# One pair of groups of the up projections token-major, parked sums in three steps, the mixing matrix loaded at another place

## The chip, the cores and the metric

The kernel runs on one core of a Trainium2 chip. The time is that of the device in microseconds (us), the median of several executions. Engines are named as in the profile: PE is TensorE's matmul stream and PEld its weight loads, DVE is VectorE, ACT is ScalarE, POOL is GpSimd and SP is SyncE. Times inside the kernel are microseconds from the start of the profiled span.

## The reference

Two layers of an encoder run over 256 tokens of width 2048 in float32. Layer 0 mixes tokens with a gated MLP over blocks of 128 positions, layer 1 with latent attention. Behind each mixer stands a gated MLP with a causal convolution of width 3, which is where most of the change lies:

```python
def conv_ffn(x, w_up, conv_w, conv_b, w_down):      # D_FF = 5504
    h = x @ w_up                                      # 256 x 2048 by 2048 x 11008
    C = h.shape[-1]
    h = lax.conv_general_dilated(h, conv_w[:, None, :], window_strides=(1,),
                                 padding=[(CONV_W - 1, 0)],
                                 dimension_numbers=('NWC', 'WIO', 'NWC'),
                                 feature_group_count=C) + conv_b
    a, g = jnp.split(h, 2, axis=-1)
    return (jax.nn.silu(g) * a) @ w_down

# token mixer of layer 0, the part with the mixing matrix w
w = w_s * mask[None]                                  # 8 matrices of 128 x 128, masked by blocks of 64
s = jnp.einsum('gij,bnjgd->bnigd', w, v) + jnp.transpose(b_s)[None, None, :, :, None]
return (u * s.reshape(B, S, GM_HALF)) @ w_out
```

Each sub-layer is followed by x <- LayerNorm(ALPHA * x + sublayer(x)).

## The kernel before

**Weights.** All weights are read once, in chunks of 128 rows by 2048 columns of float32 (1 MB), in an order that a list `chunks` fixes for the whole kernel. A class `Feed` loads each chunk on SP's queue into one of three `raw` tiles, and splits it: ScalarE rounds it into `wh` (L127) and VectorE takes the rest, `wl` = raw - wh (L130). The parts stand in the 14 slots named `big`. TensorE multiplies with three products: the activation's high and low part by wh, and its high part by wl. `feed.next()` gives the parts of the next chunk and starts loads and splits of later ones.

**Two orientations.** In the *feature-major* form of an up group (`prod_a`, tile `up`), a weight block of 128 x 128 is the stationary side and the 256 tokens are the moving one: 512 columns for wh (high and low tokens side by side) and 256 for wl. A group has four PSUM banks of 128 features each, two for `a` and two for the gate `g`, and goes through four chunks of four blocks of 128 rows; a group of four chunks has 64 matmuls with 512 moving columns and 64 with 256. The two halves of a bank are then added (`sum_halves`, L388 on ScalarE and L390 on VectorE, tile `h`), convolved (tile `c`, L960 to L963) and gated (tile `act`, L978), a pair of `a` and `g` at a time. In the *token-major* form (`prod_b`, used by the gated mixer's v and u stages, class `Banks`) 128 tokens are the stationary side and 512 weight columns move. There a chunk has two blocks of rows by 1024 columns and is either "wide" (`eight`, 24 matmuls of 512 columns) or in seven products (`seven`, 21 matmuls). The latter is Strassen's scheme in Winograd's form: ScalarE and VectorE make sums `ts` of the weight's quarters (L137) and split them into `th` and `tl` (L127, L130), and the activations have sums of their own (`combine`). `rest` puts the banks together at the end. The eight PSUM banks of such a group are q3, p2, e, q4 (`DIRECT`) and p1, q5, p7, p6 (`OWN`).

**Up projections.** Group 0 of a layer is a special one (`upf`), and groups 1 to 21 follow in a loop over `gi`, with chunks in sequence. Beside them run other jobs, taken up at fixed places in the loop: the gates of the group before, the making of the down projection's activation sums, and the *parked sums*. Of eight chunks per layer of the down projection the parts in seven products are made ahead, during the up groups: `park` loads the chunk (`praw`) on POOL's queue, makes its two pairs of parts on ScalarE and VectorE (tiles `pwh`, `pwl`, `pth`, `ptl`) and stores them to DRAM (`kept...`). It is a generator and does one step per call of `next(jobs)`. The tiles come from the six slots named `side`.

**Order.** The program is written in an order which a scheduler turns into one sequence per engine. `pin` keeps an instruction in the order of the program; `behind` puts one after the last matmul written so far, in the scheduler's order, with no semaphore. The engines then wait for each other only where data or buffers ask for it.

**The start.** TensorE runs ten warm-up matmuls over a tile `idle` of zeros. The v stage begins as soon as the first half of chunk 0 is there. The mixing matrix is loaded on POOL's queue in four tiles `wT` (L811), each followed by a clear of its masked quarter (L812), and is first used by the row sums at 52 us.

## Time and profile before

| what | value |
|---|---|
| median of 3 executions | 2463.76 us (2462.9 to 2464.14) |
| the profiled execution | 2463.38 us, span 2461.6 us |
| granted TensorE clock | 1.000 |
| busy: PE, DVE, ACT, POOL | 2453.6, 2071.6, 1498.8, 110.6 us |
| up groups 1 to 21, layer 0 and layer 1 | about 807 to 1275 us and 1767 to 2235 us |
| groups 8 and 9, layer 0 and layer 1 | 968.90 to 1013.35 us and 1928.96 to 1973.41 us |
| v stage (token-major) | about 6 to 256 us |

In the profile's lists a group of instructions is given as line, engine, operation, output<-inputs, shapes and count, then busy time and mean duration in ns, then the idle time of the engine before them and what ended it. In lists by time, the first two columns are start and length in us, and idle time stands in brackets. Matmuls overlap: one with 512 moving columns lasts 0.39 us, while the next starts 0.227 us after it.

### The profile page before, as it was taken

The numbers are of one execution on the slowest core, as the hardware profiler recorded it, in microseconds if no ns is written. First come the engines' busy times: TensorE is split into PE (matmuls) and PEld (weight loads), VectorE is DVE, ScalarE is ACT, GpSimd is POOL, SyncE is SP. The second block draws the span as 40 slices with busy tenths as digits, with TensorE's granted clock in tenths as the row PEclk, the third lists the DMA queues.
The fourth block names the chain that finished last, engine by engine and source line by source line (L and its number), as shares of the span: only waits on it lengthen the run. The fifth ranks groups of instructions, "written<-read, shape, count | busy, mean of one in ns | idle before, by whom it ended". The sixth has DMA issues, their size and how long they took to land. (4 is left out here: it accounts for less than half of the span.)

```text
span 2461.6 us, 32571 instructions
## 1 busy us (share of the span) xinstructions
PE 2453.6 (100%) x12475; PEld 2087.7 (85%) x12475; DVE 2071.6 (84%) x2739; ACT 1498.8 (61%) x2024; POOL 110.6 (4%) x214
## 2 busy tenths in 40 slices
PE   9999999999999999999999999999999999999999
PEld 7888888888888888888888888988888888888887
DVE  7999889989898788787777897868797787878798
ACT  6666777766466656656554566665665565555453
POOL 0000000000000000000001000000000000000000
PEclk9999999999999999999999999999999999999999
DMA  7556665658776778777868885443578787877885
GB/s 285 196 206 215 230 200 192 221 169 310 239 273 240 258 276 330 282 276 304 318 226 316 301 303 186 173 171 126 205 282 309 261 317 292 295 265 281 297 322 202
DMA packets 118156, 624.52 MB, mean 254 GB/s; under 512 B 10840, under 2 KB 11104, under 8 KB 75376
## 3 DMA queue, kind: packets, MB, share of 16 engines
q1 hardware_dynamic: 90128, 462.47, 53.1%
q0 software_dynamic: 27872, 159.97, 17.0%
q8 instruction: 98, 1.61, 0.3%
q14 instruction: 58, 0.48, 0.1%
HBM read 551.04 MB, written 71.35 MB: 253 GB/s over the span
## 5 line engine op out<-in xcount | busy, mean ns | idle before, releaser
L130 DVE TENSOR_TENSOR wl<-raw,wh 128x1024 fp32r<-128x1024 f32 (+4 forms) x643 | 954.5, 1499 | 155.5 <-ACT wh L127 107.5
L127 ACT CAST wh<-raw 128x1024 fp32r<-128x1024 f32 (+4 forms) x643 | 804.6, 1275 | 319.2 <-PE up L232 90.1
L232 PE MATMUL up<-xhl,wh 128*128 128x512 f32 x2624 | 611.4, 390 | 0.0
L232 PEld LDWEIGHTS up<-xhl,wh 128*128 128x128 f32 x2624 | 487.6, 188 | 97.5
L232 PEld LDWEIGHTS up<-xhl,wl 128*128 128x128 f32 x2624 | 325.8, 192 | 6.4
L232 PE MATMUL up<-xhl,wl 128*128 128x256 f32 x2624 | 328.1, 283 | 0.0
L127 ACT CAST th<-ts 128x1536 fp32r<-128x1536 f32 (+1 forms) x156 | 161.3, 1050 | 127.5 <-DVE ts L137 98.3
L130 DVE TENSOR_TENSOR tl<-ts,th 128x1536 fp32r<-128x1536 f32 (+1 forms) x156 | 184.7, 1224 | 18.1 <-PE ub L232 8.1
L232 PE MATMUL ub<-wh,xhl 128*128 128x512 f32 x516 | 161.1, 393 | 0.0
L232 PEld LDWEIGHTS ub<-wh,xhl 128*128 128x128 f32 x516 | 96.9, 188 | 21.8 <-issue 1.9
L137 DVE TENSOR_TENSOR ts<-ts,raw 128x512 f32<-128x512 f32 x156 | 107.8, 691 | 1.7
L232 PE MATMUL ub<-wl,xhl 128*128 128x512 f32 x258 | 100.5, 390 | 0.0
L137 DVE TENSOR_TENSOR ts<-raw 128x1024 f32<-128x1024 f32 x78 | 95.4, 1223 | 2.2 <-PE ub L232 1.7
L232 PE MATMUL v_q<-wh,xhl 128*128 128x512 f32 x224 | 70.6, 391 | 1.1 <-ACT wh L127 1.1
L232 PE MATMUL v_p<-wh,xhl 128*128 128x512 f32 x192 | 59.9, 389 | 0.0
L232 PEld LDWEIGHTS ub<-wl,xhl 128*128 128x128 f32 x258 | 48.4, 188 | 10.2
L232 PEld LDWEIGHTS v_q<-wh,xhl 128*128 128x128 f32 x224 | 42.0, 188 | 11.0 <-ACT wh L127 2.5
L390 DVE TENSOR_TENSOR h_1a<-up,lo_1a 128x256 f32<-128x256 f32 x41 | 17.2, 421 | 36.0 <-ACT lo_1a L388 35.8
L390 DVE TENSOR_TENSOR h_0a<-up,lo_0a 128x256 f32<-128x256 f32 x41 | 17.3, 421 | 35.7 <-ACT lo_0a L388 35.5
L154 DVE TENSOR_TENSOR praw<-praw 128x512 f32<-128x512 f32 x64 | 44.1, 689 | 0.5
L753 ACT ACTIVATE lny<-lnt,lncol 128x128 f32<-128x128 f32 x96 | 36.4, 468 | 13.1 <-PE lnt L749 13.0
L232 PE MATMUL v_q<-wl,xhl 128*128 128x512 f32 x112 | 43.8, 391 | 0.3 <-DVE wl L130 0.3
(1934 smaller groups left out, 4466.5 us busy)
## 6 DMA issues: line engine op xcount, KB each, us to landing
raw<-in_ffn_up_dram SPq DMA_DIRECT2D x172, 1024.0 KB, 7.0
raw<-in_gm_in_dram SPq DMA_DIRECT2D x93, 1024.0 KB, 5.4
raw<-in_ffn_dn_dram SPq DMA_DIRECT2D x68, 1024.0 KB, 6.9
raw<-in_gm_wout_dram SPq DMA_DIRECT2D x48, 1024.0 KB, 6.1
praw<-in_ffn_dn_dram POOLq DMA_DIRECT2D x16, 1024.0 KB, 14.6
keptth<-pth POOLq DMA_DIRECT2D x16, 1024.0 KB, 8.1
kepttl<-ptl POOLq DMA_DIRECT2D x16, 1024.0 KB, 8.9
fth<-keptth POOLq DMA_DIRECT2D x16, 1024.0 KB, 9.7
```

What stands on the lines that cost most here:

```text
L127: cast = self.nc.scalar.copy(hi, raw)
L130: self.nc.vector.tensor_tensor(lo, raw, hi.bitcast(F32), ALU.subtract)
L137: add = lambda o, a, b: self.nc.vector.tensor_tensor(o, a, b, ALU.add)
L154: add = lambda o, a, b: pin(nc.vector.tensor_tensor(o, a, b, ALU.add))
L232: recent[0] = nc.tensor.matmul(o, l, r, start=start, stop=stop, skip_group_check=True)
L390: nc.vector.tensor_tensor(h, acc[:, 0:S], lo, ALU.add)
L753: nc.scalar.activation(y[:, j], t[:, j * P : (j + 1) * P], AF.Identity, bias=lncol[:, o : o + 1], scale=lncol[:, g : g + 1])
```

## The change

It has three parts, the first in both layers.

1. Groups 8 and 9 of the up projections become one token-major group (`token_group`). Its eight chunks are cut from the same weights as two blocks of rows by 1024 columns, in the order `UP_PAIRS`; four of them (pairs 2, 3, 4, 6) are done in seven products. The sums of the activations that this needs are made in groups 5 and 6 (`sum_acts`, six rows on VectorE per pair of row blocks). The results stand with tokens on the partitions; `rest` and four additions bring them to SBUF, and 16 transposes per layer behind group 10's first chunk (`turn_group`) turn them into four banks `upr` of features. The gates of both groups then run in group 10 (`gate_group`).
2. A parked sum takes three steps, not four: its load (`ask`) is issued in the step before, behind the last one's additions. No step is taken in the group before the token-major one, one at the token-major group's first chunk, and one at the last chunk of group 10.
3. The code that loads the mixing matrix stands behind chunk 4 of the v stage and no more behind chunk 3, and its loads are put `behind` the last matmul written.

```diff
--- before.py
+++ after.py
@@ -53,6 +53,9 @@
 U_SEVEN = [(2, 3)] + [(2, 3, 4, 6)] * 4 + [(2, 3, 4)]
 
 MO_SEVEN = (1, 2)
+UP_TOKEN = (8,)
+UP_PAIRS = (0, 2, 1, 3, 5, 4, 6, 7)
+UP_SEVEN = (2, 3, 4, 6)
 
 T1, T2 = 6, 6
 SLOTS = {"big": 14, "raw": 3, "side": 6}
@@ -147,7 +150,14 @@
         self.sums = last if i >= 96 else None
         return wh, wl, th, tl
 
-    def park(self, i):
+    def ask(self, i):
+
+        ap = self.chunks[i][0]
+        raw = self.pool.tile([P, 2048], F32, tag="side", name=f"praw{i}", bufs=SLOTS["side"])
+        self.pin(self.nc.gpsimd.dma_start(raw.rearrange("p (k c) -> p k c", k=ap.shape[1]), ap))
+        return raw
+
+    def park(self, i, raw, coming, later):
 
         nc, pin = self.nc, self.pin
         tile = lambda n, dt: self.pool.tile([P, 2048], dt, tag="side", name=f"{n}{i}", bufs=SLOTS["side"])
@@ -159,10 +169,6 @@
             pin(nc.gpsimd.dma_start(d, t[:, 0:cols].bitcast(F32)))
             kept[n] = d
 
-        ap = self.chunks[i][0]
-        raw = tile("praw", F32)
-        pin(nc.gpsimd.dma_start(raw.rearrange("p (k c) -> p k c", k=ap.shape[1]), ap))
-        yield
         for n, o, cols in (("w", 512, 1536), ("t", 0, 2048)):
             hi, lo = tile(f"p{n}h", F32R), tile(f"p{n}l", F32R)
             pin(nc.scalar.copy(hi[:, 0:cols], raw[:, o : o + cols]))
@@ -176,6 +182,8 @@
                 add(r[0], r[0], r[2])
                 add(r[2], r[2], r[1])
                 add(r[3], r[3], r[2])
+                if later is not None:
+                    coming.append(self.ask(later))
                 yield
 
     def fetch(self, i):
@@ -266,14 +274,27 @@
                     parked.append(len(chunks))
                 chunks.append((w[2 * u : 2 * u + 2, :, c].rearrange("k p c -> p k c"), 2048, kind))
 
+    def up(layer):
+
+        for gi in range(22):
+            if gi - 1 in UP_TOKEN:
+                continue
+            if gi not in UP_TOKEN:
+                chunks.extend((ffn_up[layer, i], 2048, "") for i in range(4 * gi, min(4 * gi + 4, n_up)))
+                continue
+            for p in UP_PAIRS:
+                i = 4 * gi + p // 2
+                w = ffn_up[layer, i : i + 5 : 4, :, p % 2 * 1024 : p % 2 * 1024 + 1024].rearrange("f p c -> p f c")
+                chunks.append((w, 2048, "seven" if p in UP_SEVEN else "wide"))
+
     back(gm_wout, NF_GM)
-    chunks += [(ffn_up[0, i], 2048, "") for i in range(n_up)]
+    up(0)
     back(ffn_dn[0], NF_FF)
     chunks += [(ml_q[i], 2048, "") for i in range(4)]
     chunks += [(ml_kv[i], 3 * KVR, "") for i in range(5)] + [(ml_kv[5, :, 0:KVR], KVR, "")]
     chunks += [(ml_b[i], 2048, "") for i in range(ml_b.shape[0])]
     chunks += [(ml_out[i], 2048, "seven" if i - 8 in MO_SEVEN else "") for i in range(ml_out.shape[0])]
-    chunks += [(ffn_up[1, i], 2048, "") for i in range(n_up)]
+    up(1)
     back(ffn_dn[1], NF_FF)
 
 
@@ -804,11 +825,11 @@
                 nc.sync.dma_start(rope_sb, ropes)
                 nc.sync.dma_start(lnrow, ln_rows.rearrange("r (k p) -> (r k) p", p=P))
                 nc.sync.dma_start(brow[0:NG, :], b_s.rearrange("o (g i) -> (o g) i", g=NG))
-            if c == 3 and gi == 0:
+            if c == 4 and gi == 0:
                 wTg = []
                 for i in range(4):
                     t = tp.tile([P, 2, P], F32, tag="t1", name=f"wT{i}", bufs=T1)
-                    nc.gpsimd.dma_start(t, w_sT[:, 2 * i : 2 * i + 2, :])
+                    behind(nc.gpsimd.dma_start(t, w_sT[:, 2 * i : 2 * i + 2, :]))
                     nc.gpsimd.memset(t[64:P, :, 0:64], 0.0)
                     wTg += [t[:, 0, :], t[:, 1, :]]
         vt = slot([P, 2, 1024], f"v{gi}", tag="side")
@@ -903,8 +924,11 @@
 
     def park_all(until):
 
-        for i in [i for i in parked if feed.used < i < until]:
-            yield from feed.park(i)
+        line = [i for i in parked if feed.used < i < until]
+        coming = [feed.ask(line[0])]
+        yield
+        for i, later in zip(line, line[1:] + [None]):
+            yield from feed.park(i, coming.pop(0), coming, later)
             yield
 
     for g in range(6):
@@ -993,16 +1017,74 @@
         boundary(ln, acc, end, f"upf{layer}_", after)
         xhl, old = ln.new, ln
         jobs = park_all(feed.used + 2 * n_up)
+        sums, rooms, turning = {}, [], []
+
+        def sum_acts(p):
+
+            if len(sums) % 2 == 0:
+                rooms.append(slot([P, 2, 8 * P], f"xs{layer}_{p}", F32R, "side" if len(rooms) < 2 else "big"))
+            t = xhl[p // 2][:, 2 * (p % 2) : 2 * (p % 2) + 2]
+            raw = tp.tile([P, 2, S], F32, tag="t2", name=f"xr{layer}_{p}", bufs=T2)
+            nc.vector.tensor_tensor(raw, t[:, :, 0:S].bitcast(F32), t[:, :, S : 2 * S].bitcast(F32), ALU.add)
+            sums[p] = combine(f"{layer}_{p}", rooms[-1][:, len(sums) % 2, :], raw[:, 0], raw[:, 1])
+
+        def token_group(gi):
+
+            acc = Banks(f"upt{layer}_{gi}", DIRECT + OWN)
+            for c, p in enumerate(UP_PAIRS):
+                a = [[x_parts(xhl, 2 * p + j, b) for j in range(2)] for b in range(2)]
+                got = feed.next()
+                if c == 0:
+                    next(jobs, None)
+                if p in UP_SEVEN:
+                    acc.seven(a, sums[p], *got, turned=512, across=True)
+                    if p == [q for q in UP_PAIRS if q in UP_SEVEN][-1]:
+                        rest = acc.rest()
+                else:
+                    acc.eight(a, *got, across=True)
+            for n, t in zip(DIRECT, rest):
+                nc.vector.tensor_tensor(t, acc.acc[n], t, ALU.add)
+            turning.append((gi, rest, [bank(f"upr{layer}_{gi}_{i}") for i in range(4)]))
+
+        def turn_group():
+
+            gi, rest, t = turning[0]
+            for i, r in enumerate(rest):
+                b, f = i // 2, i % 2
+                for j in range(4):
+                    o = (j % 2) * S + b * P
+                    nc.tensor.transpose(t[2 * f + j // 2][:, o : o + P], r[:, j * P : (j + 1) * P], ident)
+
+        def gate_group(f):
+
+            gi, rest, t = turning[0]
+            for j in range(2):
+                c = slice(j * S, (j + 1) * S)
+                pair(2 * (gi + f) + j, t[2 * f][:, c], t[2 * f + 1][:, c])
+            if f == 1:
+                turning.pop()
+
         for gi in range(1, 22):
+            if gi - 1 in UP_TOKEN:
+                continue
+            if gi in UP_TOKEN:
+                token_group(gi)
+                continue
             nt, nk = (4, 4) if gi < 21 else (2, 8)
             acc = [bank(f"up{layer}_{gi}_{f}") for f in range(nt)]
             for c in range(KD // nk):
                 hi, lo = feed.next()
                 prod_a(acc, xhl, range(nk * c, nk * c + nk), hi, lo)
-                if gi > 1 and c in (1, 2) and gi + c > 3:
+                if gi > 1 and gi + 1 not in UP_TOKEN and c in ((3,) if gi - 2 in UP_TOKEN else (1, 2)) and gi + c > 3:
                     next(jobs, None)
                 if (gi, c) in FIRST:
                     acts.make(*plan(NF_FF)[0][FIRST.index((gi, c))])
+                if turning and c == 0:
+                    turn_group()
+                if turning and c in (1, 2):
+                    gate_group(c - 1)
+                if gi in (5, 6) and c % 2 and len(sums) < len(UP_SEVEN):
+                    sum_acts(UP_SEVEN[len(sums)])
                 if gi == 1 and c == 0:
                     after(1, 1, None)
                     for f in range(2):
```

The place where the pair begins, on TensorE. Tiles `up_8_*` are group 8's banks, `upt_8_*` those of the token-major group, `xhl` the activations; the numbers behind the names are those of the tile. Before:

```order
L232 MATMUL up_7_3_7420<-xhl_3_5824,wh_7461 128x512
L232 MATMUL up_8_0_7631<-xhl_0_5821,wh_7509 128x512
L232 MATMUL up_8_1_7632<-xhl_0_5821,wh_7509 128x512
L232 MATMUL up_8_2_7633<-xhl_0_5821,wh_7509 128x512
L232 MATMUL up_8_3_7634<-xhl_0_5821,wh_7509 128x512
L232 MATMUL up_8_0_7631<-xhl_0_5821,wh_7509 128x512
L232 MATMUL up_8_1_7632<-xhl_0_5821,wh_7509 128x512
```

And changed:

```order
L240 MATMUL up_7_3_7472<-xhl_3_5824,wh_7513 128x512
L240 MATMUL upt_8_q_7677<-wh_7553,xhl_0_5821 128x512 x2
L240 MATMUL upt_8_q_7677<-wl_7554,xhl_0_5821 128x512
L240 MATMUL upt_8_q_7677<-wh_7553,xhl_0_5821 128x512 x2
L240 MATMUL upt_8_q_7677<-wl_7554,xhl_0_5821 128x512
L240 MATMUL upt_8_p_7678<-wh_7553,xhl_0_5821 128x512 x2
L240 MATMUL upt_8_p_7678<-wl_7554,xhl_0_5821 128x512
L240 MATMUL upt_8_p_7678<-wh_7553,xhl_0_5821 128x512 x2
L240 MATMUL upt_8_p_7678<-wl_7554,xhl_0_5821 128x512
```

The stationary side was the weight and is now the activation, since an output<-inputs row names the stationary side last here: wide chunks have rows of three products for each bank, row block and block of tokens. The pair of groups had 256 such matmuls, and now it has 180.

The transposes, on TensorE, in group 10, between the last product of its first chunk with wl and the first of its second one:

```order
L240 MATMUL up_10_2_7974<-xhl_0_5821,wl_7895 128x256
L240 MATMUL up_10_3_7975<-xhl_0_5821,wl_7895 128x256
L1056 MATMUL upr_8_0_7968<-ident,upt_8w 128x128 x2
L1056 MATMUL upr_8_1_7969<-ident,upt_8w 128x128 x2
L1056 MATMUL upr_8_2_7970<-ident,upt_8p_7923 128x128 x2
L1056 MATMUL upr_8_3_7971<-ident,upt_8p_7923 128x128 x2
L1056 MATMUL upr_8_0_7968<-ident,upt_8d 128x128 x2
L1056 MATMUL upr_8_1_7969<-ident,upt_8d 128x128 x2
L1056 MATMUL upr_8_2_7970<-ident,upt_8u 128x128 x2
L1056 MATMUL upr_8_3_7971<-ident,upt_8u 128x128 x2
L240 MATMUL up_10_0_7972<-xhl_1_5822,wl_7933 128x256
L240 MATMUL up_10_1_7973<-xhl_1_5822,wl_7933 128x256
```

All 16 stand in one row, two for each of the rows shown; they read what `rest` and the additions left.

VectorE at the end of the token-major group, with three of its last four chunks (`wl` of 2048 is a wide chunk, the rows of `ts`, `wl` of 1536 and `tl` one in seven products):

```order
L133 TENSOR_TENSOR wl_7761<-raw_7689,wh_7760 128x2048
L140 TENSOR_TENSOR ts_7790<-raw_7737 128x1024
L140 TENSOR_TENSOR ts_7790<-ts_7790,raw_7737 128x512
L133 TENSOR_TENSOR wl_7792<-raw_7737,wh_7791 128x1536
L140 TENSOR_TENSOR ts_7790<-ts_7790,raw_7737 128x512
L133 TENSOR_TENSOR tl_7794<-ts_7790,th_7793 128x1536
L133 TENSOR_TENSOR tl_7794<-ts_7790,th_7793 128x512
L140 TENSOR_TENSOR ts_7827<-raw_7764 128x1024
L140 TENSOR_TENSOR ts_7827<-ts_7827,raw_7764 128x512
L133 TENSOR_TENSOR wl_7829<-raw_7764,wh_7828 128x1536
L140 TENSOR_TENSOR ts_7827<-ts_7827,raw_7764 128x512
L133 TENSOR_TENSOR tl_7831<-ts_7827,th_7830 128x1536
```

Where a chunk had two rows `wl` of 1024, a chunk in seven products has six rows.

POOL at the start. Before:

```order
L346 MEMSET epsc 128x1
L811 DMA wT_311<-in_w_sT_dram 128x256
masks.py:199 ISA
masks.py:199 AFFINE_SELECT ident<-ident 128x128
L347 MEMSET epsc 64x1
L812 MEMSET wT_311 64x2x64
L811 DMA wT_314<-in_w_sT_dram 128x256
L811 DMA wT_317<-in_w_sT_dram 128x256
L811 DMA wT_320<-in_w_sT_dram 128x256
```

And changed:

```order
L367 MEMSET epsc 128x1
masks.py:199 ISA
masks.py:199 AFFINE_SELECT ident<-ident 128x128
L368 MEMSET epsc 64x1
L832 DMA wT_348<-in_w_sT_dram 128x256
L832 DMA wT_351<-in_w_sT_dram 128x256
L832 DMA wT_354<-in_w_sT_dram 128x256
L832 DMA wT_357<-in_w_sT_dram 128x256
L833 MEMSET wT_348 64x2x64
```

The first load of `wT` has moved back behind the fill of `ident` and the last `epsc`, and the other three have moved ahead of the first clear.

## The prediction

> **What bounds the kernel now.** I read the page's busy shares first, then TensorE's own waits, then the chain of waits in the up projections, since an edit of matmuls pays in full only where TensorE itself sets the end.
>
> ```profile
> PE 2453.6 (100%) x12475; PEld 2087.7 (85%) x12475; DVE 2071.6 (84%) x2739; ACT 1498.8 (61%) x2024; POOL 110.6 (4%) x214
> PE warm L232 <- POOL idle L283: 1.3, 1, 1.3
> PE v_q L232 <- ACT wh L127: 1.1, 2, 0.9
> PE v_q L232 <- DVE wl L130: 0.3, 1, 0.3
> ...
> PE upf L232 <- ACT xhl L756: 0.2, 1, 0.2
> 1779.12 450.10 PE up L232 x2592
> ```
>
> TensorE is busy for 2453.6 of 2461.6 us. Its waits are tiny, and the only ones near an edit are the two of v_q, both in the first 20 us. The last row is one piece of the chain: all up groups of layer 1, 2592 matmuls in a row with no other engine between. A matmul taken out there shortens the run by its cadence, as long as VectorE, at 84%, still delivers the split weights in time. So there are three questions: what TensorE saves, whether VectorE carries the added work, and what the start-up does.
>
> **TensorE: what goes.** Groups 8 and 9 have 128 matmuls with a moving side of 512 and 128 with 256, per layer. The windows over exactly this stretch, layer 0 and layer 1, columns as PE, PEld, DVE, ACT, POOL busy, clock, DMA share and GB/s:
>
> ```profile
> 968.90:1013.35 44.45, 44.45 (x258) 39.38 (x257) 34.42 (x49) 25.87 (x37) 2.87 (x5) 1.00 0.69 256
> 1928.96:1973.41 44.45, 44.45 (x257) 39.38 (x256) 34.04 (x49) 25.79 (x37) 2.86 (x5) 1.00 0.69 256
> ```
>
> 44.45 us go. The chain agrees: 450.10 / 2592 x 256 = 44.45.
>
> **What comes.** Eight token-major chunks: four with 24 matmuls of 512, four in seven products with 21, 180 in all. The v stage already has this mix, and three such blocks of 180 read:
>
> ```profile
> 93.78:134.58 40.80, 40.80 (x182) 33.80 (x180) 39.61 (x37) 27.28 (x33) 0.00 (x0) 1.00 0.58 206
> 134.58:175.38 40.80, 40.80 (x182) 33.79 (x180) 39.52 (x37) 27.28 (x33) 0.00 (x0) 1.00 0.58 207
> 175.38:216.18 40.80, 40.80 (x182) 33.80 (x180) 39.61 (x37) 27.27 (x33) 0.00 (x0) 1.00 0.58 206
> ```
>
> 40.80 us without a gap, 227 ns each, although VectorE is 97% busy. Then 16 transposes of 128x128 come in, which turn the token-major sums. The u stage has 16 of them in a row between matmuls; the third row is after them:
>
> ```profile
> 316.96 1.91 PE L901 MATMUL ub<-ident,v 128*128 128x128 f32 x16
> 318.63 0.71 PE L232 MATMUL ub<-wh,xc 128*128 128x512 f32 x2
> 319.17 0.39 PE L232 MATMUL ub<-wl,xc 128*128 128x512 f32 x1
> L991 PE MATMUL uph<-ident,upt x16: 272/272/273, 806.8 to 1778.8; 128*128 128x128 f32 x16
> ```
>
> From start to start the 16 take 318.63 - 316.96 = 1.67 us, 104 ns each. The next two matmuls take 0.54 instead of 2 x 0.227, so 0.09 more: 1.76 us in all. The last row gives one transpose's whole duration, 272 ns, the upper end if nothing overlapped: 16 x 0.272 = 4.35 us. I take 1.76, since the nearest row is the same form 16 times in a row on a full TensorE. The Trainium skill ("TensorE: Matmul & The Clock Gate", Part 4: PE-mode transpose) gives some 275 ns for a transpose inside a kernel and says that it doesn't count as busy for the clock gate. The trace agrees with that length for one alone, but not as a price in a row. By its 275 ns the sum would lose 2.6 us per layer, the third rival below.
>
> Per layer: 44.45 - 40.80 - 1.76 = 1.89 us; both layers 3.78. The bounds for this term are 3.78 and 2 x (44.45 - 40.80 - 4.35) = -1.40.
>
> **VectorE: does it keep up?** Costs of its work per eight chunks come from the groups of the v stage, which hold three such blocks. Its pitch is below the duration: three splits of 1.22 us in a row took 3.49 us.
>
> ```profile
> L130 DVE TENSOR_TENSOR wl<-raw,wh 128x2048 fp32r<-128x2048 f32 x12 | 27.2, 2290 | 0.9 <-issue 0.4
> L130 DVE TENSOR_TENSOR tl<-ts,th 128x1536 fp32r<-128x1536 f32 x12 | 21.1, 1756 | 1.0 <-PE v_p L232 0.8
> L130 DVE TENSOR_TENSOR wl<-raw,wh 128x1536 fp32r<-128x1536 f32 x12 | 21.0, 1753 | 1.3 <-PE v_q L232 1.3
> L137 DVE TENSOR_TENSOR ts<-ts,raw 128x512 f32<-128x512 f32 x25 | 17.2, 690 | 0.5
> L137 DVE TENSOR_TENSOR ts<-raw 128x1024 f32<-128x1024 f32 x12 | 14.7, 1221 | 0.0
> L130 DVE TENSOR_TENSOR tl<-ts,th 128x512 fp32r<-128x512 f32 x12 | 8.2, 686 | 0.0
> 811.23 3.49 DVE L130 TENSOR_TENSOR wl<-raw,wh 128x1024 fp32r<-128x1024 f32 x3
> L961 DVE SCALAR_TENSOR_TENSOR c_0a<-h_0a,cst,c_0a 128x255 f32<-128x255 f32 x22 | 10.6, 481 | 8.0 <-ACT c_0a L960 7.9
> L390 DVE TENSOR_TENSOR h_0a<-up,lo_0a 128x256 f32<-128x256 f32 x23 | 9.7, 421 | 21.2 <-ACT lo_0a L388 21.0
> L169 DVE TENSOR_TENSOR ptl<-praw,pth 128x2048 fp32r<-128x2048 f32 x6 | 13.7, 2286 | 0.3 <-ACT pth L168 0.3
> ```
>
> Splits: (27.2 + 21.1 + 21.0 + 17.2 + 14.7 + 8.2) / 3 = 36.5 us by durations. In the changed order there stand between them 6 h, 12 convolution steps, 4 act (priced as h) and one ptl, the gates of groups 6 and 7 and a park step: 6 x 0.42 + 12 x 0.48 + 4 x 0.42 + 2.29 = 12.3. That is 48.8 over 51 instructions; less 0.085 us of overlap each (1.22 against the pitch (3.49 - 1.22) / 2 = 1.135) it is 44.5 us, against 40.8 of TensorE. So VectorE falls back by 3.7 us. Ahead of it, groups 5 and 6 get the sums of four activation pairs (per pair two adds of 512 and four of 128, some 2.0 us) and denser park steps, which now need three calls and not four per sum. What the lead is now:
>
> ```profile
> 902.20:924.40 22.20, 22.20 (x129) 19.69 (x128) 19.41 (x28) 14.78 (x20) 1.09 (x2) 1.00 0.56 201
> 924.40:946.70 22.30, 22.30 (x130) 19.73 (x130) 18.72 (x26) 14.52 (x20) 1.78 (x3) 1.00 0.97 361
> 946.70:968.90 22.20, 22.20 (x130) 19.66 (x129) 18.71 (x27) 14.06 (x22) 1.09 (x2) 1.00 0.83 312
> L232 PE MATMUL up<-xhl,wl x448: 277/283/367, 816.5 to 965.1; 128*128 128x256 f32 x150
> L130 DVE TENSOR_TENSOR wl<-raw,wh x76: 1212/1220/2293, 745.0 to 964.7; 128x1024 fp32r<-128x1024 f32 x70, 128x2048 fp32r<-128x2048 f32 x5, 128x1536 fp32r<-128x1536 f32 x1
> L232 PE MATMUL upf<-wl,xhl x32: 389/393/476, 787.7 to 813.8; 128*128 128x512 f32 x32
> ```
>
> At 968.9, TensorE has used 448 / 16 + 32 / 8 = 32 up chunks, and VectorE has split 70 / 2 = 35. So it leads by three chunks, 3 x 22.2 / 4 = 16.7 us. Group 5 goes from 19.4 to about 25 and falls 3 us back, group 6 lands near its 22.3, group 7 (no sums and no park step) regains all of it, the pair loses 3.7, and group 10, with two more pairs of gates but no h for them, regains that too. The lowest lead is some 12 us, so I put the stalls at 0. What is thin is something else: all eight PSUM banks belong to the token-major group, so its late products (p7, p6) wait for the h of group 7, which now stand on VectorE behind two splits and behind group 6's gates. My walk along the two orders leaves them only about 1 us. Bounds for the stalls: 0, and 3.7 + 3.0 per layer if there were no lead at all. The other additions hide behind TensorE: four results of 512 and four adds at the group's end run while group 10's first bank-free matmuls go, ScalarE loses eight rows at 61%, and the loads keep their 1 MB per chunk at a DMA share of 0.58 to 0.69.
>
> **The parked sums.** Same loads, splits and stores, asked for one step earlier and done in fewer groups: VectorE work moved, none added. Its cover is the lead above. A praw that lands late is waited for by ScalarE and VectorE, not by TensorE; now it has one more step of about 5.6 us. I cost it at 0.
>
> **The mixing matrix.** Before, POOL waits for the first load before it issues the other three:
>
> ```profile
> 1.45 0.68 POOL L811 DMA_DIRECT2D wT<-in_w_sT_dram  x1
> 8.71 0.20 POOL L812 MEMSET wT<- 64x128 f32 x1 [6.14 <-DMA wT<-in_w_sT_dram]
> 9.19 1.62 POOL L811 DMA_DIRECT2D wT<-in_w_sT_dram  x3 [0.28 <-issue]
> 9.91 0.50 PE L232 MATMUL v_q<-wh,xhl 128*128 128x512 f32 x1 [0.90 <-ACT wh L127]
> 19.88 0.50 PE L232 MATMUL v_q<-wl,xhl 128*128 128x512 f32 x1 [0.31 <-DVE wl L130]
> 2.00:20.00 18.00, 16.56 (x63) 10.84 (x62) 10.59 (x15) 8.78 (x13) 2.90 (x10) 1.00 1.00 367
> ```
>
> In the changed order the four loads stand together ahead of all the clears, so one issues about 1 us later and three do so some 4 to 6 us earlier, at 2.6 to 6 us: later in the code is mostly earlier on the queue. The DMA engines are full (share 1.00). Three loads of 128 KB at 367 GB/s are 1.07 us that now compete with the weights for which TensorE stops at 9.91, less 0.36 us for the first one. But the second stop, at 19.88, hangs on a later weight load, and by then the same bytes have moved in both orders, so a delay at 9.91 is mostly absorbed there. I take +0.2; bounds -1.2 (both waits gone, 0.90 + 0.31) and +0.9. A rule that speaks for the loss is in the Trainium skill ("DMA: Bandwidth & Descriptors", Queues, rings and completion order): each engine takes turns between the queues by packet, so the extra queue would take its share at once.
>
> **Sum.** -3.78 + 0.2 + 0 = -3.6 us on the profiled execution (2463.38, span 2461.6). It lies 0.38 below the median of 2463.76; from that median the forecast is 2460.2.
>
> **The rivals.**
> *VectorE or the banks hold TensorE up.* For it: 44.5 us of work against 40.8 and the 1 us at p7 and p6. Against it: a lead of 16.7 us, and the v stage without a gap at 97%. It decides once the lead is under 3.7 us. With no lead: 2 x 6.7 = 13.4 us, so 2473.6, slower. With 0.5 to 3 us per layer at the banks alone: 2461 to 2466.
> *The start-up gains.* Both v_q waits go because POOL no longer interleaves: -1.2 instead of +0.2, 2458.8. For it: the three loads at 9.19 stood ahead of the weight for the stop at 19.88. Against it: full DMA engines.
> *The transposes don't overlap.* 4.35 per layer: 2463.76 + 1.40 + 0.2 = 2465.4. Against it: the row of 16 in 1.91 us.
>
> **Chances.** Forecast 0.62, stalls at the banks 0.15, VectorE in full 0.10, start-up gain 0.08, transposes 0.05. 0.2%, about what can be told from no change, is 4.9 us: below 2458.8 is faster, above 2468.7 slower. The start-up rival lies on the first edge, which with the forecast's tail gives faster 0.08; VectorE in full gives slower 0.10; the rest, 0.82, is the same. The range takes the forecast, the bank stalls, the transposes and the edge of the start-up: 2458.8 to 2466.0.
>
> **What would show it.** Each step right: the pair with its transposes at 42.6 us and TensorE without idle time, 16 transposes within 1.7 us start to start, VectorE at 97% or more in the pair, the wT loads issued together before 7 us, the stop at 8.6 us longer and that at 19 us shorter. Wrong: waits of upt or up rows on DVE h, tl or wl, or on the adds at the group's end; a pair of over 44.45 us means that nothing is won.

## The result, and the profile after

The median is 2458.40 us (13 executions, 2457.32 to 2459.82) against 2463.76 us of the kernel before, measured beside it (13 executions, 2461.95 to 2465.04): ratio 0.9979, 95% interval 0.9971 to 0.9987, 5.4 us less. In two later series the changed kernel lay 4.6 us (2458.63 against 2463.18) and 5.7 us (2457.93 against 2463.61) below the kernel before. The forecast was 2460.2 in a range from 2458.8: the sign was right, the gain was larger than every sum made for it, and the range ended 0.4 us too high. That miss is smaller than the 1.1 us between the three series.

The profiled execution took 2457.95 us with a span of 2455.8. Its busy times on the page:

```profile
PE 2449.0 (100%) x12355; PEld 2079.4 (85%) x12355; DVE 2121.6 (86%) x2811; ACT 1511.0 (62%) x2018; POOL 110.4 (4%) x214
```

and TensorE's waits (total, times, longest):

```profile
PE warm L240 <- POOL idle L304: 1.3, 1, 1.3
PE v_q L240 <- ACT wh L130: 0.5, 1, 0.5
PE fin L240 <- DVE dg L751: 0.3, 1, 0.3
PE upf L240 <- ACT xhl L777: 0.2, 1, 0.2
```

There are 120 matmuls fewer (2 x (256 - 196)) and VectorE works 50 us more. Two waits are gone from the list: v_q on wl at the start, and dn_q on wl, which belongs to the last down projection, far behind the pairs. In the list of the kernel before it reads:

```profile
PE dn_q L232 <- DVE wl L130: 0.2, 1, 0.2
```

The edited stretch, by windows over the token-major group and over group 10 with the transposes, layer 0 and then layer 1; columns as before:

```profile
967.90:1008.87 40.97, 40.97 (x182) 33.61 (x181) 38.73 (x42) 25.73 (x28) 1.09 (x2) 1.00 0.65 218
1008.87:1032.80 23.93, 23.93 (x145) 21.41 (x144) 23.37 (x40) 16.52 (x24) 0.66 (x2) 1.00 0.67 246
1925.60:1966.60 41.00, 41.00 (x182) 33.66 (x181) 38.72 (x42) 26.14 (x29) 1.09 (x2) 1.00 0.65 218
1966.60:1990.60 24.00, 24.00 (x146) 21.44 (x145) 23.42 (x40) 16.13 (x24) 0.71 (x2) 1.00 0.67 243
```

A feature-major group takes 22.23 us, so the transposes cost 23.93 - 22.23 = 1.70, and the pair with them 40.97 + 1.70 = 42.67 us, against 44.45 before and 42.56 in the forecast. TensorE is busy without a gap, and VectorE is busy for 95% of the token-major group (38.73 of 40.97 us) and 98% of group 10. By the same windows layer 1 takes 42.77 us, so the pair saves 1.7 to 1.8 us per layer.

To see where the rest comes from, each matmul that both profiles have (all but the pair's) was matched by its tiles, and the difference of its start (after minus before) was followed through the span. It changes only at few places: to -1.04 us in the first 20 us; by -1.71 at layer 0's pair; by -0.1 in its down projection (1404 us); by -0.08 at 1665 us; by -0.34 at 1733 us, at the end of the attention's output projection; by -1.80 at layer 1's pair; by -0.19 at 2364 us and by -0.52 at 2434 us, in the last down projection. The sum is -5.8, which is the difference of the spans. So 3.5 us are the pairs, 1.0 the start, and 1.2 stand at small waits that no edit touches. Of these, the 0.1 at 1404 us is no effect of the change: it shows as well when the unchanged kernel is profiled a second time (-0.11), and so may the 0.08 at 1665 us, where that second profile moves nearly as much. The other three make 1.05 us.

The start, on POOL and on TensorE:

```profile
1.82 1.75 POOL L832 DMA_DIRECT2D wT<-in_w_sT_dram  x3
6.05 0.54 POOL L832 DMA_DIRECT2D wT<-in_w_sT_dram  x1 [2.48 <-PE warm L240]
6.26 0.50 PE L240 MATMUL v_q<-wh,xhl 128*128 128x512 f32 x1 [0.51 <-ACT wh L130]
18.84 0.50 PE L240 MATMUL v_q<-wl,xhl 128*128 128x512 f32 x1
```

The loads do stand before 7 us. But the stop that ended at 9.9 us (the prediction's stop at 8.6, by the matmul ahead of it) is not longer, it is gone, and the one at 19 us has shrunk to 0.11 us of delay.

### The profile page after: what moved, and what is told of

Same layout as the page of the kernel before. It is cut to its first block, busy times and chain, and to the rows that moved or that the text cites. A ratio compares the mean times of both kernels' runs of the same rounds, so it can differ in the third digit from the quotient of the medians.

```text
span 2455.8 us, 32403 instructions
## 1 busy us (share of the span) xinstructions
PE 2449.0 (100%) x12355; PEld 2079.4 (85%) x12355; DVE 2121.6 (86%) x2811; ACT 1511.0 (62%) x2018; POOL 110.4 (4%) x214
## 5 line engine op out<-in xcount | busy, mean ns | idle before, releaser
L133 DVE TENSOR_TENSOR wl<-raw,wh 128x1024 fp32r<-128x1024 f32 (+4 forms) x627 | 944.9, 1524 | 131.5 <-ACT wh L130 92.1
L240 PE MATMUL up<-xhl,wh 128*128 128x512 f32 x2368 | 552.1, 390 | 0.0
L240 PEld LDWEIGHTS up<-xhl,wh 128*128 128x128 f32 x2368 | 439.8, 188 | 88.2
L240 PEld LDWEIGHTS up<-xhl,wl 128*128 128x128 f32 x2368 | 294.1, 192 | 5.8
L240 PE MATMUL up<-xhl,wl 128*128 128x256 f32 x2368 | 296.6, 283 | 0.0
L130 ACT CAST th<-ts 128x1536 fp32r<-128x1536 f32 (+1 forms) x172 | 177.9, 1050 | 146.8 <-DVE ts L140 112.6
L133 DVE TENSOR_TENSOR tl<-ts,th 128x1536 fp32r<-128x1536 f32 (+1 forms) x172 | 203.3, 1218 | 22.3 <-PE ub L240 8.2
L140 DVE TENSOR_TENSOR ts<-ts,raw 128x512 f32<-128x512 f32 x172 | 118.0, 686 | 1.8
L240 PE MATMUL mo<-wh,oT 128*128 128x512 f32 x128 | 42.8, 412 | 0.0
L240 PE MATMUL upf<-wh,xhl 128*128 128x512 f32 x128 | 42.2, 403 | 0.3 <-ACT xhl L777 0.2
```

The costliest lines, as they stand in the source:

```text
L130: cast = self.nc.scalar.copy(hi, raw)
L133: self.nc.vector.tensor_tensor(lo, raw, hi.bitcast(F32), ALU.subtract)
L140: add = lambda o, a, b: self.nc.vector.tensor_tensor(o, a, b, ALU.add)
L240: recent[0] = nc.tensor.matmul(o, l, r, start=start, stop=stop, skip_group_check=True)
```

## Experiments

Each median is compared with that of the kernel before in the same series of executions. Differences of starts are those of matched matmuls against the first profile of before, unless it is said otherwise.

### The kernel before again: what scatters by itself

No edit; a second profile of the same kernel.

> The kernel before, unchanged, for a second profile of it. If the 1.04 us of the first 20 us and the 1.2 us of small waits near 1733, 2364 and 2434 us come from the change, this profile shows them as the first one of before did: the row v_q behind the wait on wh at about 9.9 us, the wait on wl at about 19.9 us, a dn_q wait at about 2434 us; median 2463.8 +- 1. If they are only scatter between executions, they lie elsewhere or are missing here, and the span is some 1 to 2 us shorter.

Median 2463.89 against 2463.55. Its profile starts differently with the same instructions: at 20 us it stands 1.48 us ahead of the first one, so the start moves by as much as the change was thought to have gained there. It still waits in both late places, and then some:

```profile
PE warm L232 <- POOL idle L283: 1.3, 1, 1.3
PE dn_q L232 <- DVE wl L130: 0.7, 2, 0.6
PE v_q L232 <- DVE wl L130: 0.3, 1, 0.3
PE fin L232 <- DVE dg L730: 0.3, 1, 0.3
PE upf L232 <- ACT xhl L756: 0.2, 1, 0.2
PE mo_q L232 <- DVE wl L130: 0.2, 1, 0.2
```

So the 1.04 us at the start can't be booked to the change from one pair of profiles, while the late waits (mo_q, dn_q) are there in this one too.

### The three parts apart

The place of the mixing matrix's loads alone, in the kernel before:

```diff
-            if c == 3 and gi == 0:
+            if c == 4 and gi == 0:
...
-                    nc.gpsimd.dma_start(t, w_sT[:, 2 * i : 2 * i + 2, :])
+                    behind(nc.gpsimd.dma_start(t, w_sT[:, 2 * i : 2 * i + 2, :]))
```

> Only the place of the mixing matrix's loads is changed. Theory: the first wT load was issued ahead of the second half of weight chunk 0 and held it up; behind it the wait at 9.9 us shrinks by 1.0 us and the one at 19.9 us stays about half: the up projections start at 806.5 instead of 807.5 us, total -1.0 us (2462.7). Rival of the prediction: the same bytes move, +0.2 us (2464.0). Third: start scatter, no steady sign.

Median 2463.25 against 2463.55, ratio 0.9998 (0.9989 to 1.0007): nothing that can be told. Its start stood where the first profile of before stood (-0.04 us at 20 us), and the waits of mo_q and dn_q were there.

The parked sums alone, `ask` and the new `park` and `park_all` in the kernel before:

```diff
+    def ask(self, i):
...
-    def park(self, i):
+    def park(self, i, raw, coming, later):
...
+                if later is not None:
+                    coming.append(self.ask(later))
```

> Only the parked sums in three steps. TensorE's instructions are those of before. Theory (instruction fetches of 16 KB that fall into a tight weight load cause the waits at 1733 us): nothing changes there, the wait of 0.2 us stays, total within 0.3 us of before. Rival (the denser parked sums free the down projection's last chunks): the waits on dn_q near 2363 and 2434 us go, -0.7 us, while that at 1733 us stays.

Median 2463.08 against 2463.18, ratio 1.0 (0.9991 to 1.0009). The dn_q wait stayed. The small one of mo_q was gone in its profile, against the first theory; more on that below.

The token-major group and the parked sums, with the mixing matrix loaded as before (the first diff above turned round, in the changed kernel), twice:

> The token-major group and the three-step parked sums, with the mixing matrix loaded as before. Theory (three independent parts): start as before (up projections from 807.5 us), the pair with its transposes 1.7 to 1.8 us shorter per layer, total -3.5 to -4.7 us by whether the small waits near 1733 and 2434 us go as well (2459.1 to 2460.3). Rival: the start's gain belongs to the sequence of the whole program, then -5.3 us (2458.4).

> Again the pair and the parked sums with the mixing matrix loaded as before, to see whether its -6.1 us against the -4.6 and -5.4 of the whole change repeats. If moving the loads costs TensorE 0.2 us or more at the start, this stays 0.5 to 1 us under the changed kernel (2457.5); if that was scatter of the start, it lies at 2458.5.

Medians 2457.42 against 2463.55 (ratio 0.9976, 0.9967 to 0.9986) and 2458.14 against 2463.67 (0.9978, 0.9969 to 0.9987): 6.1 and 5.5 us less, which is more than either expectation of the first run. The parked sums alone gave nothing, so the whole gain comes with the token-major group. In both profiles the pairs give -1.68 to -1.77 per layer, the mo_q place -0.32 to -0.34, the places at 2364 and 2434 us together -0.58 to -0.70. The starts, with the old loads, stood at -1.44 and -0.99.

The whole change again, in two series:

> The changed kernel, unchanged, beside the others of this call. If moving the mixing matrix's loads costs or gains nothing, it lies at -6 us as the pair alone did (2457.5); if it costs 0.5 to 1 us, at -5.3 (2458.3).

> The changed kernel a third time, for the comparison in one call with the mixing matrix on SP's queue: -4.5 to -5.4 us against before (2458.2 to 2459).

Medians 2458.63 and 2457.93, 4.6 and 5.7 us below before. Their starts stood at -0.69 and -1.30. Over these profiles, the start stands at 0, -1.48 and -0.71 with the loads as in before (two of before, one of the parked sums alone), at -1.44 and -0.99 in the pair alone, and at -1.04, -0.69, -1.30 and -0.04 with the loads moved. The two sets overlap fully: moving the loads has no effect on the start that these runs can tell, and the one of 1.04 us is within the scatter.

### Is the loading of the mixing matrix worth anything?

In the changed kernel the loads go to SP's queue, where they stand behind nine chunks and the constants. Run twice:

```diff
-                    behind(nc.gpsimd.dma_start(t, w_sT[:, 2 * i : 2 * i + 2, :]))
+                    behind(nc.sync.dma_start(t, w_sT[:, 2 * i : 2 * i + 2, :]))
```

> The changed kernel with the four wT loads on SP's queue behind the weight chunks and the constants, so really later (after 25 us, their first use is at some 52 us). Theory, the first 20 us are bound by the bytes loaded: 0.5 MB less there at 370 GB/s is 1.4 us, so the two waits of v_q go wholly and it gains another 0.5 to 0.8 us over the changed kernel (2457.7). Rival, only the first wT load's place ahead of chunk 0's second half mattered: 0 to -0.2 us. A loss would come from the weight chunks behind it in SP's queue.

> Again the changed kernel with the mixing matrix on SP's queue behind the weight chunks, beside the changed kernel itself in one call. If loading it really late helps, it lies 0.5 to 1.2 us under the changed kernel (2457.3 against 2458.5), and the v stage's wait on wh at 9.9 us is gone in the trace; if its 2457.2 was scatter, both agree within 0.4 us.

Medians 2457.16 and 2457.09, against 2463.55 and 2463.61 of before and, in the second series, 2457.93 of the changed kernel. The two ratios there (0.9972, 0.9961 to 0.9983, and 0.9977, 0.9968 to 0.9986) overlap, but both series give nearly the same median, and the executions (2456.37 to 2457.63 in the second, 2456.42 to 2457.97 in the first) lie below nearly all of the changed kernel's (2457.37 to 2459.17). It is the lowest median of all versions, by 0.8 us against the changed kernel beside it, but only by 0.3 against the pair with the old loads (2457.42, in the first series). In the profiles the wait of v_q is gone, as it is in some with other loads (the third of the changed kernel, the first of the pair alone), and the starts stand at -1.94 and -1.21. Of the two mechanisms on record the one by the number of bytes fits this, but is not shown, since the second start lies inside the scatter; the other, that the first load's place ahead of chunk 0's second half is what matters, would have shown with the loads moved on POOL too, where nothing was seen.

### Where TensorE's instructions are fetched

The load that mo_q (the attention's output projection) waits for shows what differs at 1733 us. The view of the DMA queues over that load in the kernel before:

```profile
DMA packets 255, 1.88 MB, mean 284 GB/s; under 512 B 27, under 2 KB 27, under 8 KB 27
q1 hardware_dynamic: 254, 1.86, 76.4%
q8 instruction: 1, 0.02, 1.8%
raw<-in_ml_out_dram SPq DMA_DIRECT2D x2, 1024.0 KB, 7.5
```

and in the changed one, over the same load:

```profile
DMA packets 206, 1.43 MB, mean 264 GB/s; under 512 B 32, under 2 KB 32, under 8 KB 32
q1 hardware_dynamic: 206, 1.43, 72.4%
raw<-in_ml_out_dram SPq DMA_DIRECT2D x2, 1024.0 KB, 5.5
```

One instruction packet (the row q8; 16 KB, at 1719.3 us in the trace) lies among the weight's packets before, and none after. ScalarE, which casts that chunk, waits for it for 3.88 us before and 2.59 us after:

```profile
1724.35 1.05 ACT L127 CAST wh<-raw 128x1024 fp32r<-128x1024 f32 x1 [3.88 <-DMA raw<-in_ml_out_dram]
```

```profile
1720.10 1.05 ACT L130 CAST wh<-raw 128x1024 fp32r<-128x1024 f32 x1 [2.59 <-DMA raw<-in_ml_out_dram]
```

By then the change has taken 60 matmuls out of TensorE's stream, each with its weight load, so 120 instructions. A packet holds 256, and so 136 instructions more put its edges where 120 fewer do. To move the packets with no change in the work, tiny matmuls of zeros were put behind the warm-up, 68 into the kernel before:

```diff
         mm(warm, idle[:, 0:P], idle, True, True)
+    for _ in range(68):
+        mm(warm[:, 0:8], idle[:, 0:P], idle[:, 0:8], True, True)
```

> The kernel before with 68 tiny matmuls (8 columns of zeros) behind the warm-up, which shift TensorE's later instructions by 136 places, to the place where the pair's removal puts them in the latent attention's output projection. Theory of the fetches: the 16 KB instruction packet at 1719 us moves out of the weight load, that load lands about 1.2 us earlier and the wait of mo_q at 1733 us (0.2 us idle, 0.3 us in all) goes. Rival (the wait hangs on the order of work before): it stays. The start is later by the tiny matmuls and that is left out.

> Again the kernel before with 68 tiny matmuls in the start, now timed. In the trace of the first one the waits near 1733, 2363 and 2434 us were gone, -1.1 us behind the v stage, and the start was caught up by 20 us. Theory: so much is in the median, -0.7 to -1.3 us against the kernel before, with no change in any work. Rival (the start's scatter or another run takes it back): within 0.3 us of before.

The packets came at 1706.0 and 1735.1 us, outside the load, and ScalarE's wait there fell:

```profile
1723.07 1.05 ACT L127 CAST wh<-raw 128x1024 fp32r<-128x1024 f32 x1 [2.67 <-DMA raw<-in_ml_out_dram]
```

By the median differences ahead of and behind each place, the step at 1733 us was -0.35 in the first profile and -0.31 in the second. At 2364 us both lost 0.21; at 2434 us the first lost 0.56 and the second gained 0.11. The start had caught up by 20 us. The first took 2462.24 us in its one execution. The second gave a median of 2462.07 against 2463.61, ratio 0.9993 (0.9984 to 1.0002): 1.5 us less by the medians for a kernel that does slightly more work, but with an interval that contains 1.

Then the other way round, 60 tiny matmuls in the changed kernel:

> The changed kernel with 60 tiny matmuls behind the warm-up: 120 places, as many as the pair has taken away by that point, so that the instruction packets fall in the output projection where they fell before. Theory: a 16 KB packet lies inside the weight load some 14 us ahead of the stage's end, that load takes over 6 us instead of 4.9, and a wait of mo_q on wl of 0.2 us comes back. Rival: no wait, as in the changed kernel.

The packet came back into the load (at 1718.5 us), and so did ScalarE's wait:

```profile
1722.12 1.05 ACT L130 CAST wh<-raw 128x1024 fp32r<-128x1024 f32 x1 [3.77 <-DMA raw<-in_ml_out_dram]
```

TensorE lost 0.25 us at that place against the changed kernel, though in steps too small for the list of waits. The one execution took 2459.00 us.

And 128 tiny matmuls in the kernel before, a shift by one whole packet:

> The kernel before with 128 tiny matmuls, 256 instructions, which at 64 bytes each are one packet of 16 KB: the packets fall where they fall before. Theory: the fetch lies in the weight load at 1719 us (later by the start's shift) and the waits near 1733, 2363 and 2434 us stay, each within 0.15 us of the kernel before. Rival (the tiny matmuls or the later start do it, not the place of the packets): the waits go as with 68.

The packet was in the load again:

```profile
1726.60 1.05 ACT L127 CAST wh<-raw 128x1024 fp32r<-128x1024 f32 x1 [3.69 <-DMA raw<-in_ml_out_dram]
```

But TensorE did not wait at 1733 us this time (-0.15 against before), at 2364 us 0.13 was gone, and at 2434 us the wait stayed (-0.11). The start was 2.6 us later, and the one execution took 2465.43 us.

Over all 18 profiles ScalarE's wait for this load is 3.64 to 4.29 us in the seven where the packet lies in the load, and 2.46 to 2.67 us in the eleven where it does not. So that a 16 KB instruction packet makes a 1 MB weight load land 1.2 us later is shown by moving it out, in, and round by a whole packet. What TensorE pays for it is less even. The eleven all lose 0.30 to 0.37 us at this place against the first profile of before; against them the packet costs 0.25 to 0.8 us in five of the seven, and under 0.2 in two (the parked sums alone and the whole packet). Why it differs was not measured.

The steps at 2364 and 2434 us go back to one load in the same way. In the kernel before a packet starts at 2332.5 us, inside a load that ScalarE casts at 2338 us; with 68 tiny matmuls there is none:

```profile
2337.99 1.92 ACT L127 CAST wh<-raw 128x2048 fp32r<-128x2048 f32 x1 [5.23 <-DMA raw<-in_ffn_dn_dram]
```

```profile
2336.87 1.91 ACT L127 CAST wh<-raw 128x2048 fp32r<-128x2048 f32 x1 [4.48 <-DMA raw<-in_ffn_dn_dram]
```

Over the 18 profiles this wait is 5.03 to 6.17 us in the six with a packet in that load, and 4.38 to 4.65 us in the twelve without. The six are the four whose TensorE runs the matmuls of before (two of before, the loads moved alone, the parked sums alone), the shift by a whole packet, and the version with six chunks in seven products below; both profiles with 68 tiny matmuls are among the twelve. The issues of the loads on SP's queue, measured against TensorE's matmuls and compared with the first profile of before, agree to 0.01 us from 2299 to 2335 us in all profiles. From 2342 us to the kernel's last load, all come 0.58 to 0.85 us earlier in the twelve, and between 0.21 us earlier and 0.94 us later in the other five of the six. So one late load holds back every load behind it: each waits for a free `raw` tile, and none catches up. All twelve lose 0.19 to 0.21 us at 2364 us, and eleven of them 0.37 to 0.56 at 2434, where the last chunk's split is waited for; the other five lose at most 0.17 and 0.11. The twelfth is the second profile with 68: there ScalarE waited 4.00 us for the last load but one, against 3.01 in the first, and the wait at 2434 us came back. Why that load was late stays open.

### How near to its end VectorE is

Only one of the eight pairs of row blocks in seven products, and then six:

```diff
-UP_SEVEN = (2, 3, 4, 6)
+UP_SEVEN = (6,)
```

> The changed kernel with one of the eight pairs in seven products, not four, so nearly all in 24 products. TensorE: 189 matmuls of 512, 42.84 us, plus 1.76 for the transposes, against 44.45 for the two feature-major groups: the group saves nothing (+0.15 per layer), total +4.1 against the changed kernel (2462.7). VectorE in the pair falls by about 12 us. If the gain came from VectorE's or the queues' relief instead of fewer matmuls, it would stay at 2458 to 2459.

2461.83 in one execution. By windows, layer 0:

```profile
968.20:1011.10 42.90, 42.90 (x191) 35.51 (x191) 30.23 (x35) 19.36 (x23) 0.53 (x1) 1.00 0.66 233
1011.10:1035.00 23.90, 23.90 (x145) 21.40 (x144) 20.91 (x35) 14.59 (x22) 1.11 (x3) 1.00 0.55 190
```

66.80 us with group 10, against 3 x 22.23 = 66.69 of feature-major groups: the token-major form with its transposes gains nothing. The gain of the pair is that of the seven products alone. The one execution is still 1.8 us below before. By its matched starts 0.7 of that is the start, and 1.1 stands at 1733, 2364 and 2434 us, as in the changed kernel, while the pairs lose 0.1 to 0.15 each. So the late gain does not need the pair's: it comes with the number of instructions.

```diff
-UP_SEVEN = (2, 3, 4, 6)
+UP_SEVEN = (2, 1, 3, 4, 6, 7)
...
-                if gi in (5, 6) and c % 2 and len(sums) < len(UP_SEVEN):
+                if gi in (4, 5, 6) and c % 2 and len(sums) < len(UP_SEVEN):
```

> The changed kernel with six of the eight pairs of row blocks in seven products, not four. TensorE loses 6 matmuls more per layer (-1.36 us); VectorE gets 2 x 4.1 us of splits more in the pair and two more sums before. Theory (VectorE is at its end in the pair): it is short by some 12 us there, and even with three chunks of lead TensorE waits for wl, tl or the banks, 3 to 8 us per layer, so 2463 to 2472. Rival (the lead covers it as it did for four): 2456.

2471.34 in one execution, some 13 us above the changed kernel. By windows and TensorE's rows with waits in layer 0:

```profile
967.90:1014.00 46.10, 41.35 (x175) 31.61 (x173) 45.93 (x51) 28.71 (x31) 1.09 (x2) 1.00 0.52 189
```

```profile
982.55 0.70 PE L240 MATMUL upt_p<-th,xs 128*128 128x512 f32 x2 [0.94 <-DVE h_0g L411]
984.46 0.73 PE L240 MATMUL upt_q<-wh,xs 128*128 128x512 f32 x2 [0.28 <-ACT wh L130]
986.55 0.73 PE L240 MATMUL upt_q<-th,xs 128*128 128x512 f32 x2 [0.43 <-ACT th L130]
...
1008.71 0.50 PE L240 MATMUL upt_q<-th,xs 128*128 128x512 f32 x1 [1.35 <-ACT th L130]
1014.33 1.20 PE L240 MATMUL up<-xhl,wh 128*128 128x512 f32 x4 [1.92 <-ACT upt_8p L473]
```

VectorE is busy for 45.93 of 46.10 us. The first wait is the bank's, for the h of group 7, and the others are splits and the copy for `rest`, which come after it in the same queues. This is the slower rival of the prediction at its place, two chunks in seven products further on. It had been priced at 13.4 us for less work on VectorE, so that the sizes agree is in part luck.

How far the change itself is from it shows where that h stands in the changed kernel, on VectorE and on TensorE:

```profile
979.88 0.42 DVE L411 TENSOR_TENSOR h_0a<-up,lo_0a 128x256 f32<-128x256 f32 x1
981.37 0.42 DVE L411 TENSOR_TENSOR h_0g<-up,lo_0g 128x256 f32<-128x256 f32 x1
```

```profile
980.39 0.69 PE L240 MATMUL upt_p<-th,xs 128*128 128x512 f32 x2
982.06 0.63 PE L240 MATMUL upt_p<-th,xs 128*128 128x512 f32 x2
```

The banks come free at 980.30 and 981.79, and are used at 980.39 and 982.06: 0.1 and 0.3 us of margin.

A second token-major group per layer, 14 and 15, from the same activation sums, with the mixing matrix on SP's queue:

```diff
-UP_TOKEN = (8,)
+UP_TOKEN = (8, 14)
```

> The changed kernel with a second token-major group per layer, groups 14 and 15, from the same activation sums, and the mixing matrix on SP's queue. Theory (what a pair saves is TensorE time alone, 1.75 us in the trace, and VectorE carries it since the second pair needs no new sums): another -3.5 us, 2453.9. Rival (VectorE or the six side slots, two of which hold the sums until group 14, are at their end): stalls beside the second pair or in the parked sums, and a gain under 1 us or a loss against the changed kernel.

2458.45 against 2463.67, ratio 0.9979 (0.9970 to 0.9988): 5.2 us less, where one pair with the same loads gave 6.4 and 6.5. The second pair, by windows over it and over group 16, and its wait:

```profile
1098.85:1139.60 40.75, 39.87 (x172) 31.40 (x171) 37.34 (x40) 27.41 (x29) 1.09 (x2) 1.00 0.59 206
1139.60:1165.70 26.10, 26.10 (x155) 23.15 (x155) 25.33 (x41) 16.49 (x24) 0.53 (x1) 1.00 0.70 261
```

```profile
1116.98 0.73 PE L240 MATMUL upt_q<-th,xs 128*128 128x512 f32 x2 [0.78 <-ACT th L130]
```

66.85 us for three groups against 66.69: the split of a chunk in seven products came late, and what the products save went into that wait and smaller ones behind it. Another 0.8 us went at 1733 us, where the instruction packet lies in the load again (a wait of 4.29 us on ScalarE).

## Why the prediction was wrong, by its steps

**TensorE's term held.** 3.78 us were forecast for the two pairs, 3.5 were measured. 40.97 and 41.00 us stand against 40.80, and the transposes took 1.70, against 1.76. The nearest row, 16 transposes on a full TensorE, was the right one; the price by 272 ns each, and the rival made of it, are out: four took 0.60 us, and the next four began 0.43 later.

```profile
1014.40 0.60 PE L1056 MATMUL upr<-ident,upt_8w 128*128 128x128 f32 x4
1014.83 0.60 PE L1056 MATMUL upr<-ident,upt_8p 128*128 128x128 f32 x4
1015.27 0.60 PE L1056 MATMUL upr<-ident,upt_8d 128*128 128x128 f32 x4
1015.71 0.60 PE L1056 MATMUL upr<-ident,upt_8u 128*128 128x128 f32 x4
1016.06 1.20 PE L240 MATMUL up<-xhl,wl 128*128 128x256 f32 x8
```

The Trainium skill's some 275 ns ("TensorE: Matmul & The Clock Gate", Part 4: PE-mode transpose) is near the length of one, 272 ns in the trace of before, and not the price in a row.

**VectorE carried it, but not with the lead that was named.** The stalls came out at 0 as taken. The lead of three chunks did not: at 967.9 us the splits stood two chunks ahead, some 10 us at 5.1 us a chunk, where "the lowest lead is some 12 us" was named. A chunk in seven products fills five of the 14 slots, which may be the reason; no run tests it. VectorE's work ahead of the pair was also put too high:

```profile
901.20:923.50 22.30, 22.30 (x130) 19.72 (x130) 20.32 (x29) 16.77 (x23) 0.53 (x1) 1.00 0.78 294
923.50:945.70 22.20, 22.20 (x130) 19.66 (x128) 21.03 (x30) 14.26 (x22) 2.31 (x4) 1.00 1.00 393
```

Groups 5 and 6 came to 20.3 and 21.0 us (the third busy time of a row), not 25 and 22.3. In the pair VectorE was busy for 95%, not the 97% that was to be the sign. The margin of about 1 us for the late products was 0.1 to 0.3 us, so the conclusion held by less than the prediction thought. The two chunks more in seven products, and the second pair, show how close it was: the rival was placed rightly.

**The parked sums** gave nothing, as taken.

**The mixing matrix** was given +0.2 us with bounds from -1.2 to +0.9, on the ground that three loads compete with the weights. Alone it can't be told from nothing. The step failed where it took the profile's own start as the start: two profiles of the same kernel differ there by 1.48 us. The rival of the start-up comes nearest to the result, at 2458.8 us, but by number only: its mechanism gave nothing when it was tested alone.

**What failed is the sum's silent term: all of the program outside the edits was taken as unchanged.** About 1.0 us of the gain stands at three waits, 390 to 720 us behind the nearest pair. Fewer matmuls move the places where TensorE's instructions are fetched, and a packet leaves two loads that were late by it: one ahead of 1733 us (0.34 us), and one at 2338 us, from which the steps at 2364 and 2434 us follow (0.19 and 0.52). Moving the packets alone, in the kernel before, took these steps away, all three in one profile and two in the other. That the packets left just these loads is luck of the count: with a second pair one came back into the first of them. The rest of the distance, from 4.5 to the 4.6 to 5.7 us measured, lies in the scatter of the start and of the last down projection (before once lost 0.7 us more at 2364 us, where the load at 2338 us landed later still) and is not settled. The range was too narrow for the same reason: it was drawn from the bounds of the terms alone and left out that a profile of the same kernel scatters by more than 1 us at places that the median contains.

## What to carry to other kernels

Price an edit of a full TensorE by the row that stands in the same company (16 transposes in a row, a block of the same product mix): two such rows came out to within 0.2 us. Take a second profile of the unchanged kernel before a difference of 1 us at the start is booked to an edit. And when the instruction count changes, look at every tight load behind it for instruction packets, since a kernel can gain or lose there with no change in its work.

## What the runs showed of the hardware

TensorE's instructions are fetched in packets of 16 KB: 98 in the trace of before, 15 to 36 us apart, counted among the 16 DMA engines' packets like the weights. It has 12475 matmuls and as many weight loads, so some 64 bytes for each. One packet took 0.9 to 2.1 us, and a weight load of 1 MB in which it fell kept ScalarE waiting for 3.6 to 4.3 us where it was 2.5 to 2.7 without it, in another place for 5.0 to 6.2 us where it was 4.4 to 4.7. 128 matmuls more ahead of it, 256 instructions, brought the packets back into the same loads.
